# Three products of two tiles per f on GpSimd in an MLP of a hybrid encoder layer, and a later split of the first chunk's gated tiles

## The chip, the core and the metric

The kernel runs on one core of a Trainium2 chip. Five engines work side by side, each with its own queue of instructions that it takes in order: TensorE (PE, matmuls; PEld are its weight loads), VectorE (DVE), ScalarE (ACT), GpSimd (POOL) and SyncE (SP, which only issues DMAs here). They wait for each other through semaphores. The metric is the device time of one execution in microseconds (us).

## The reference

One encoder layer over 512 tokens of width 2048: a normalised input projection, a convolution group and a neighbourhood-attention group beside each other, an output projection, and then a gated MLP. The change touches the MLP alone:

```python
xn = rms_norm(x, ffn_norm_g[l])
up = jnp.einsum("bsd,df->bsf", xn, w_up[l])
up = depthwise_conv(up, ffn_dw_w[l], ffn_dw_b[l])     # width 3 over tokens
gate, val = jnp.split(up, 2, axis=-1)
x = x + jnp.einsum("bsf,fd->bsd", jax.nn.silu(gate) * val, w_down[l])
return rms_norm(x, final_norm_g)
```

D_FF is 5632, so `up` has 11264 columns. All data are float32.

## The kernel before

Everything is kept transposed: a tile has 128 channels as partitions and 512 tokens as columns. A float32 product is made of matmuls on a rounded high part and a low part of each operand (`hi`/`lo`, `hh`/`hl`): `mm3` (L122 to L127) issues high by high (L125), high by low (L126) and low by high (L127). For each weight unit of 128x1024, `parts` (L111) makes the high part on ACT (`whi`, L114) and the low part on DVE (`wlo`, L115); there are four buffers of each, and SP loads the raw units into seven buffers.

The MLP runs over f = 0 to 43 (`NF`), each f standing for 128 columns of gate and 128 of value. Four f make a chunk (`CH` = 4), so there are eleven chunks c. For each f, `up` (or `up_apart` in chunk 0) makes seven products, numbered 0 to 6, instead of eight, in the manner of Strassen-Winograd: the weights of a product are sums of the raw units (`factors`, DVE adds `ws`, L622 to L633), and the products are added up to g and v from PSUM (`pu`) on ACT and DVE (L684 are ACT's copies `vv` and `pl` out of a bank). Products 0 to 5 share three PSUM banks (`psm`), so product 3 takes the bank of product 0; product 6 has its own (`po`).

`hidden(f)` (L764) then multiplies g and v by the reciprocal norm `rstd2` (L766, L767), runs the convolution (`conv3`: L758 on ACT, L759 and L760 on DVE, each for g and v), the silu (L769, ACT), and the gated product (L770). `in_two` (L773) splits a gated tile into `hh` (L775, ACT) and `hl` (L776, DVE). The first three gated tiles of a chunk are split just before the last f of the chunk, the fourth at the end of the chunk.

A chunk's gated tiles go through the down projection during the next chunk: `up` calls `between` after each product, and after products 3 and 6 `down` (L779) multiplies the four tiles of the chunk before with a unit of down weights, two output tiles d at a time (`pd`). ACT copies each result out (`pdc`, L790) and GpSimd issues a DMA that adds it to `x2d` in DRAM (L791).

The order on each engine is not the order of the source. The program is written with priorities, and a scheduler with its own costs orders each engine's instructions when the kernel is built. Each engine then keeps to this fixed order, so an instruction that waits holds up all that stand behind it on its engine.

At the very end of the kernel four products of final tiles run on GpSimd (L839) beside DVE's (L841); until then GpSimd's work is DMA issues.

Of the kernel before, what the change touches and what calls it, by code (L numbers as in the profile page):

```python
# [41 lines left out]
CH = 4  # L42
# [23 lines left out]
def layer(ctx: ExitStack, tc: tile.TileContext, xT, w_in, w_out, w_up, w_down, par, tab, out):  # L66
    nc = tc.nc
# [16 lines left out]
    def t2(name, dt=F32):  # L84
        return tp.tile([P, S], dt, tag="t2k", name=name)
# [174 lines left out]
    for k in range(KD):  # L260
        x1.append(t2("x"))
        last = pin(nc.sync.dma_start(x1[k], xT[k]))
        h, l = t2("xh", F32R), t2("xl", F32R)
# [8 lines left out]
    for step in ORDER:  # L272
        i = next(a_ if step == "a" else q_)
# [323 lines left out]
    rstd2 = []  # L597
# [44 lines left out]
    def down_units(c, i, at):  # L642

        n = U // CH
        if not c:
            return ()
        if c < NCH - 1:
            return {3: (4 * i,), 6: (4 * i + n,)}.get(at, ())
        return {(1, 3): (0,), (1, 6): (2,), (2, 3): (4,), (2, 6): (6,), (3, 6): range(8, KD, n)}.get((i, at), ())
# [104 lines left out]
    def conv3(a, n):  # L754
        y = t2("uy")
        o = POFF["fww"] + 3 * n
        w, o = (prm, o) if n < NF else (fwn, o - POFF["fww"] - 3 * NF)
        nc.scalar.activation(y, a, AF.Identity, scale=w[:, o + 1:o + 2], bias=pc("fwb", n))  # L758
        nc.vector.scalar_tensor_tensor(y[:, 1:], a[:, :S - 1], w[:, o:o + 1], y[:, 1:], op0=ALU.mult, op1=ALU.add)  # L759
        nc.vector.scalar_tensor_tensor(y[:, :S - 1], a[:, 1:], w[:, o + 2:o + 3], y[:, :S - 1],  # L760
                                       op0=ALU.mult, op1=ALU.add)
        return y

    def hidden(f, between):  # L764
        g, v = (up_apart if f < CH else up)(f, between)
        nc.vector.tensor_mul(g, g, rstd2[0])  # L766
        nc.vector.tensor_mul(v, v, rstd2[0])  # L767
        g, v = conv3(g, f), conv3(v, NF + f)
        nc.scalar.activation(g, g, AF.Silu)  # L769
        nc.vector.tensor_mul(g, g, v)  # L770
        return g

    def in_two(g):  # L773
        h, l = t2("hh", F32R), t2("hl", F32R)
        nc.scalar.activation(h, g, AF.Copy)  # L775
        nc.vector.tensor_sub(l, g, h.bitcast(F32))  # L776
        return h, l

    def down(hs, ds, wide=False):  # L779

        for d0 in ds:
            w = weights()
            for d in range(d0, d0 + U // CH):

                ps = (psm.tile([P, S], F32, tag="mm", name="pd") if wide and d % 5 > 1 else
                      psa.tile([P, S], F32, tag="tr", name="pd", bufs=2))
                for k in range(CH):
                    mm3(ps, w, (d - d0) * CH + k, *hs[k], k == 0, k == CH - 1)
                t = t2("pdc")
                nc.scalar.activation(t, ps, AF.Copy)  # L790
                nc.gpsimd.dma_start(xd[d], t, accum_op=ALU.add)  # L791

    pend = None
    for c in range(NCH):
        hs = []
        for i in range(CH):

            last = c == NCH - 1 and i == CH - 1
            if i == CH - 1:
                hs = [in_two(h) for h in hs]  # L800
            hs.append(hidden(c * CH + i, lambda at: None if last else down(pend, down_units(c, i, at))))
        hs[-1] = in_two(hs[-1])
        if not last:
            pend = hs

# [141 lines left out]
```

## Time and profile before

| | us |
|---|---|
| three runs | 2051.95, 2054.8, 2055.14 |
| median | 2054.8 |
| the profiled execution, its own time | 2052.8 |
| its span, first to last instruction | 2051.0 |
| PE in the products of chunk 0 (f = 0 to 3), from the span's start | 682 to 766 |
| PE in those of chunks 1 to 10, with the down projection of chunks 0 to 9 | 766 to 1988 |

How to read what is shown of it. A row of the table of waits says which engine, writing which tile at which line, waited for which engine's tile: total us, times, longest. A row of a group says line, engine, operation, the tiles out<-in, shapes and count, then busy us and mean ns of one, then the engine's idle time ahead of them and what ended it. A row of the timeline begins with its start and duration in us; brackets at its end hold the idle time before it and what ended it. The row by windows has the length of the stretch and then, for PE, PEld, DVE, ACT and POOL, busy us and instructions, then the granted clock. `source` rows give min/median/max in ns. Matmuls are pipelined, so their durations overlap and the step from start to start tells their rate.

### The profile page before, as it was taken

What the parts mean: (1) busy time and instruction counts of PE and PEld (TensorE: products, weight loads), DVE (VectorE), ACT (ScalarE), POOL (GpSimd) and SP (SyncE); (2) the same over time, 40 slices, a digit from 0 to 9 for tenths busy, and PEclk for the clock granted to TensorE, in tenths of its full rate; (3) what the DMA queues carried; (4) which work ended last, traced back from release to release, by engine and by line L of the source; (5) the groups of instructions that cost most, each with busy time, mean ns of one, the idle gap of its engine ahead of it and who ended that gap; (6) DMA issues with size and microseconds to landing.
All of it is one profiled execution on the core that took longest, in us unless ns stands there. A gap on an engine that the chain in (4) does not pass through costs nothing.

```text
span 2051.0 us, 28588 instructions
## 1 busy us (share of the span) xinstructions
PE 2031.7 (99%) x10816; PEld 1736.7 (85%) x10816; DVE 1666.7 (81%) x2319; ACT 1060.8 (52%) x1726; POOL 156.2 (8%) x186
## 2 busy tenths in 40 slices
PE   9999999999999999999999999999999999999997
PEld 7888888888788998888888888888888888888887
DVE  7996697686577898888878878888888888889876
ACT  6244424457436555555555555555554555555562
POOL 0000000000001001111111111111111111110110
PEclk9999999999999999999999999999999999999999
DMA  7332333236237435555555565565565565555682
GB/s 253 113 103 83 99 98 111 84 103 237 82 118 184 119 116 130 135 149 136 129 147 141 128 145 143 129 143 144 124 144 144 124 150 141 136 129 134 147 212 83
DMA packets 97209, 275.38 MB, mean 134 GB/s; under 512 B 10928, under 2 KB 11696, under 8 KB 97072
## 3 DMA queue, kind: packets, MB, share of 16 engines
q1 hardware_dynamic: 71712, 227.40, 35.0%
q0 software_dynamic: 25216, 46.15, 14.8%
q8 instruction: 85, 1.39, 0.3%
q14 instruction: 52, 0.43, 0.1%
q10 hardware_dynamic: 144, 0.01, 0.0%
HBM read 218.99 MB, written 54.53 MB: 133 GB/s over the span
## 4 chain that ended last, share of the span: by engine, by line
PE 97%; DVE 1%; DMA 0%; issue 0%; ACT 0%; DVEq 0%; ACTq 0%
PE pu L672 25%; PE pu L677 13%; PE pd L127 8%; PE pd L125 8%; PE pd L126 8%; PE pj L125 7%; PE pj L127 7%; PE pj L126 7%; PE po L125 3%; PE po L127 3%; PE po L126 3%; PE pu L125 1%; PE pu L127 1%; PE pu L126 1%; PE sc L437 1%; PE po L476 1%
## 5 line engine op out<-in xcount | busy, mean ns | idle before, releaser
L114 ACT ACTIVATE whi<-raw 128x1024 fp32r<-128x1024 f32 x364 | 384.4, 1058 | 486.8 <-PE pj L126 178.5
L115 DVE TENSOR_TENSOR wlo<-raw,whi 128x1024 fp32r<-128x1024 f32 x364 | 444.3, 1222 | 221.4 <-ACT whi L114 198.8
L672 PE MATMUL pu<-xc,whi 128*128 128x512 f32 x2240 | 574.7, 392 | 0.0
L672 PEld LDWEIGHTS pu<-xc,whi 128*128 128x128 f32 x2240 | 409.1, 189 | 74.0 <-ACT pl L684 0.2
L677 PEld LDWEIGHTS pu<-xc,wlo 128*128 128x128 f32 x2240 | 305.6, 190 | 21.9
L677 PE MATMUL pu<-xc,wlo 128*128 128x256 f32 x2240 | 312.3, 282 | 0.0
L125 PE MATMUL pd<-hh,whi 128*128 128x512 f32 x640 | 249.0, 391 | 2.6 <-ACT hh L775 2.6
L125 PE MATMUL pj<-xh,whi 128*128 128x512 f32 x640 | 251.1, 396 | 0.0
L127 PE MATMUL pj<-xh,wlo 128*128 128x512 f32 x640 | 249.7, 390 | 0.0
L126 PE MATMUL pj<-xl,whi 128*128 128x512 f32 x640 | 249.7, 390 | 0.0
L126 PE MATMUL pd<-hl,whi 128*128 128x512 f32 x640 | 249.2, 389 | 0.0
L127 PE MATMUL pd<-hh,wlo 128*128 128x512 f32 x640 | 249.2, 391 | 0.0
L791 POOL DMA_DIRECT2D x2d<-pdc x160 | 139.3, 872 | 1167.7 <-ACT pdc L790 949.5
L684 ACT ACTIVATE pl<-pu 128x256 f32<-128x256 f32 x280 | 104.5, 382 | 166.0 <-PE pu L672 165.9
L114 ACT ACTIVATE whi<-ws 128x1024 fp32r<-128x1024 f32 x132 | 139.8, 1059 | 78.1 <-PE pu L672 57.9
L343 DVE SCALAR_TENSOR_TENSOR y<-ch,prm,y 128x504 f32<-128x504 f32 (+14 forms) x240 | 173.7, 742 | 4.6
L115 DVE TENSOR_TENSOR wlo<-ws,whi 128x1024 fp32r<-128x1024 f32 x132 | 161.0, 1220 | 19.8 <-ACT whi L114 19.7
L127 PEld LDWEIGHTS pd<-hh,wlo 128*128 128x128 f32 x640 | 120.1, 188 | 28.8 <-DVE wlo L115 3.0
L125 PEld LDWEIGHTS pj<-xh,whi 128*128 128x128 f32 x640 | 120.2, 188 | 27.9 <-issue 3.7
L127 PEld LDWEIGHTS pj<-xh,wlo 128*128 128x128 f32 x640 | 120.2, 188 | 25.9 <-DVE wlo L242 0.4
L126 PEld LDWEIGHTS pj<-xl,whi 128*128 128x128 f32 x640 | 120.4, 188 | 25.0 <-DVE xl L265 0.7
L125 PEld LDWEIGHTS pd<-hh,whi 128*128 128x128 f32 x640 | 120.5, 188 | 24.9 <-ACT hh L775 3.0
(182 smaller groups left out, 2742.9 us busy)
## 6 DMA issues: line engine op xcount, KB each, us to landing
raw<-in_w_up SPq DMA_DIRECT2D x176, 512.0 KB, 3.6
raw<-in_w_down SPq DMA_DIRECT2D x88, 512.0 KB, 3.7
x2d<-pdc POOLq DMA_DIRECT2D x160, 256.0 KB, 4.7
raw<-in_w_in SPq DMA_DIRECT2D x76, 512.0 KB, 3.7
raw<-in_w_out SPq DMA_DIRECT2D x32, 512.0 KB, 3.9
x<-in_xT SPq DMA_DIRECT2D x32, 256.0 KB, 5.3
tab<-in_tab SPq DMA_DIRECT2D x32, 256.0 KB, 5.2
x2d<-x SPq DMA_DIRECT2D x16, 256.0 KB, 2.1
```

What stands on the lines that cost most here:

```text
L114: i = nc.scalar.activation(hi[:, :n], raw[:, :n], AF.Copy)
L115: j = nc.vector.tensor_sub(lo[:, :n], raw[:, :n], hi[:, :n].bitcast(F32))
L125: nc.tensor.matmul(ps, hi[:, a], mh, start=start, stop=False)
L126: nc.tensor.matmul(ps, hi[:, a], ml, start=False, stop=False)
L127: return nc.tensor.matmul(ps, lo[:, a], mh, start=False, stop=stop)
L343: nc.vector.scalar_tensor_tensor(y[:, a:b], h[:, a + j - PAD:b + j - PAD], prm[:, o + j:o + j + 1], y[:, a:b], op0=ALU.mult, op1=ALU.add)
L437: m = nc.tensor.matmul(banks[b // 2 * 2 + j][:, b % 2, :], q[hp, b * P:(b + 1) * P], grid(k, KC0[b], KW)[hp], start=True, stop=True)
L476: m = nc.tensor.matmul(grid(po, b * BLK, BLK)[hp], vt[b // 2][:, 2 * (b % 2) + ch, hp], pts[b // 2 * 2 + j][:, 2 * (b % 2) + ch, :], start ...
L672: return nc.tensor.matmul(ps, w[0][:, k * P:(k + 1) * P], comb[c][k], start=k == 0, stop=k == U - 1)
L677: nc.tensor.matmul(ps[:, H:], w[1][:, k * P:(k + 1) * P], comb[c][k][:, :H], start=False, stop=False)
L684: nc.scalar.activation(to, ps, AF.Copy)
L791: nc.gpsimd.dma_start(xd[d], t, accum_op=ALU.add)
```

## The change

```diff
     def hidden(f, between):
         g, v = (up_apart if f < CH else up)(f, between)
-        nc.vector.tensor_mul(g, g, rstd2[0])
-        nc.vector.tensor_mul(v, v, rstd2[0])
+        mul = (nc.gpsimd if f >= CH and f % CH < CH - 1 else nc.vector).tensor_mul
+        mul(g, g, rstd2[0])
+        mul(v, v, rstd2[0])
         g, v = conv3(g, f), conv3(v, NF + f)
         nc.scalar.activation(g, g, AF.Silu)
-        nc.vector.tensor_mul(g, g, v)
+        mul(g, g, v)
         return g
...
         for i in range(CH):
 
             last = c == NCH - 1 and i == CH - 1
-            if i == CH - 1:
+            if c and i == CH - 1:
                 hs = [in_two(h) for h in hs]
             hs.append(hidden(c * CH + i, lambda at: None if last else down(pend, down_units(c, i, at))))
-        hs[-1] = in_two(hs[-1])
+        hs = [h if isinstance(h, tuple) else in_two(h) for h in hs]
         if not last:
             pend = hs
```

From f = 4 on, the two products with the norm and the gated product of an f run on GpSimd, except in the last f of a chunk, where they stay on DVE. That is 30 f and 90 products of 128x512. In chunk 0 all products stay on DVE, and the first three gated tiles are split at the end of the chunk together with the fourth. One line is added ahead of the products, so lines from L766 on have a number higher by one in the changed kernel.

The scheduler orders the changed program anew. PE has the same instructions; their order differs at ten places, after product 2 of the last f of chunks 1 to 9 and at the first down projection after chunk 0. At the nine, eight down matmuls stood between products 2 and 3, and now three do; the other five come after product 3. On ACT, the copies L684 of products 0 and 1 there now come directly behind the `hh` of the third gated tile, ahead of a `whi`. On GpSimd the products stand between the accumulations of `x2d`.

## The prediction

> **What bounds the kernel now.** I read the page first, then the table of PE's waits, then the groups by line and shape, then the timeline at the places that the waits point to. Times of the timeline are microseconds from the span's start.
>
> ```profile
> span 2051.0 us, 28588 instructions
> PE 2031.7 (99%) x10816; PEld 1736.7 (85%) x10816; DVE 1666.7 (81%) x2319; ACT 1060.8 (52%) x1726; POOL 156.2 (8%) x186
> PE 97%; DVE 1%; DMA 0%; issue 0%; ACT 0%; DVEq 0%; ACTq 0%
> ...
> PE pd L125 <- ACT hh L775: 2.6, 1, 2.6
> ...
> PEld pd L127 <- DVE wlo L115: 3.0, 9, 0.3
> ...
> 820.00:1960.00 1140.00, 1140.00 (x5997) 979.95 (x5996) 957.81 (x1210) 625.97 (x979) 127.05 (x146) 1.00 0.56 138
> ```
>
> PE sets the end: 97% of the chain is matmuls, and from 820 to 1960, which is nearly all of the MLP from f = 4 on, PE is busy for all of 1140 us at the full granted clock (1.00), while DVE works 957.81. DVE can therefore cost time only where PE waits for it. The waits name two such places in the MLP: once 2.6 us for a high part (hh) of a gated tile, and nine times for a low part of down weights (wlo). Nine is the number of full chunks after the first (c = 1 to 9). Whatever the change saves on DVE, no more can be won here than these two waits hold.
>
> The nine waits look alike. This is the one in the middle of chunk 3, where f%4 is 3:
>
> ```profile
> 1102.53 0.87 POOL L791 DMA_DIRECT2D x2d<-pdc  x1 [9.45 <-ACT pdc L790]
> ...
> 1105.11 1.23 DVE L115 TENSOR_TENSOR wlo<-raw,whi 128x1024 fp32r<-128x1024 f32 x1 [2.13 <-ACT whi L114]
> ...
> 1105.46 0.80 ACT L758 ACTIVATE uy<-g,prm 128x512 f32<-128x512 f32 x1
> ...
> 1110.03 0.74 DVE L760 SCALAR_TENSOR_TENSOR uy<-vl,fwn,uy 128x511 f32<-128x511 f32 x1
> ...
> 1110.69 0.68 DVE L776 TENSOR_TENSOR hl<-uy,hh 128x512 fp32r<-128x512 f32 x1
> ...
> 1111.29 0.69 DVE L770 TENSOR_TENSOR uy<-uy 128x512 f32<-128x512 f32 x1
> 1111.89 1.22 DVE L115 TENSOR_TENSOR wlo<-raw,whi 128x1024 fp32r<-128x1024 f32 x1
> 1112.01 0.64 ACT L775 ACTIVATE hh<-uy 128x512 fp32r<-128x512 f32 x1 [0.97 <-DVE uy L770]
> ...
> 1112.41 0.40 PE L125 MATMUL pd<-hh,whi 128*128 128x512 f32 x1
> ...
> 1112.61 1.06 ACT L114 ACTIVATE whi<-raw 128x1024 fp32r<-128x1024 f32 x1
> 1112.64 0.39 PE L126 MATMUL pd<-hl,whi 128*128 128x512 f32 x1
> ...
> 1113.17 0.50 PE L127 MATMUL pd<-hh,wlo 128*128 128x512 f32 x1
> ...
> 1113.57 0.36 ACT L684 ACTIVATE vv<-pu 128x256 f32<-128x256 f32 x1
> ...
> 1113.84 0.37 ACT L684 ACTIVATE pl<-pu 128x256 f32<-128x256 f32 x1
> ...
> 1114.43 0.63 PE L672 MATMUL pu<-xc,whi 128*128 128x512 f32 x2
> ```
>
> PE runs eight down matmuls (pd) here between product 2 and product 3 of an f. They step by 0.23 (1112.41 to 1112.64), so eight take 1.84; they took 2.02 (to 1114.43), because L127 waited for the wlo that ended at 1113.11. The stall is 0.18 at each border, 1.6 over nine. Two more things matter below. Product 3 needs the bank of product 0, which ACT frees with the two L684 copies at 1113.57 and 1113.84 (done 1114.21, only 0.22 before PE takes it); and these copies stand behind hh in ACT's queue.
>
> The single wait is the border after chunk 0:
>
> ```profile
> 766.18 1.22 DVE L115 TENSOR_TENSOR wlo<-raw,whi 128x1024 fp32r<-128x1024 f32 x1
> ...
> 767.42 7.23 SPq L109 DMA_DIRECT2D raw<-in_w_up  x2
> ...
> 771.94 1.23 DVE L622 TENSOR_TENSOR ws<-raw 128x1024 f32<-128x1024 f32 x1 [1.33 <-DMA raw<-in_w_up]
> ...
> 774.38 0.40 PE L125 MATMUL pd<-hh,whi 128*128 128x512 f32 x1
> ...
> 776.20 0.75 DVE L760 SCALAR_TENSOR_TENSOR uy<-vl,fwn,uy 128x511 f32<-128x511 f32 x1
> ...
> 776.44 0.39 PE L125 MATMUL pd<-hh,whi 128*128 128x512 f32 x1
> ...
> 779.40 0.50 PE L125 MATMUL pd<-hh,whi 128*128 128x512 f32 x1 [2.57 <-ACT hh L775]
> ```
>
> PE stood from 776.67 to 779.40, 2.73 us. The end of an L115 frees the buffer whose load starts at 767.42; L622 waits for that load, and the convolution and the last gated tile queue behind L622.
>
> **The change part by part.** *Removed from DVE.* Thirty f (three in each of chunks 1 to 10) lose three products each:
>
> ```profile
> L766 DVE TENSOR_TENSOR g<-g,rstd 128x512 f32<-128x512 f32 x44 | 30.4, 691 | 1.3
> L770 DVE TENSOR_TENSOR uy<-uy 128x512 f32<-128x512 f32 x44 | 30.2, 686 | 0.1
> ...
> L839 POOL TENSOR_TENSOR fin<-x,rb x4: 718/720/726, 2042.2 to 2044.3; 128x256 f32<-128x256 f32 x4
> ...
> L841 DVE SCALAR_TENSOR_TENSOR fin<-x,prm,rb 128x256 f32<-128x256 f32 x12 | 4.8, 476 | 0.9 <-PE rb L201 0.9
> ...
> L722 DVE TENSOR_TENSOR g<-vv,pu 128x256 f32<-128x256 f32 x40 | 16.6, 415 | 0.0
> ```
>
> 90 x 0.69 = 62 us less for DVE, worth nothing by itself under a PE that is busy throughout.
>
> *Added to GpSimd.* No row has a 128x512 product there. At 128x256 it takes 0.72. DVE's own pair, 415 ns at 256 and 690 at 512, has a fixed part of 140; with that, GpSimd gets 0.14 + 2 x 0.58 = 1.30. Bounds: 0.72 (all of it fixed) and 1.44 (none). I take 1.30: 90 of them add 117 us to 127 us of work in a stretch of 1140, so GpSimd does not become the bound.
>
> *Where GpSimd's products wait and who waits for them.* In GpSimd's queue the product of g stands behind one x2d accumulation: free at 1103.40, done at 1104.70, and ACT's L758, its reader, starts only at 1105.46. So this is covered by 0.76, without interference. The product of v comes earlier still. DVE idles 2.13 just before 1105.11, which takes up one delay of 1.30. The x2d issues that queue behind a product go out up to 1.3 later; the next accumulation on the same x2d is a chunk away.
>
> *The third product at a border.* The gated products of f%4 = 0 and 1 are split only when f%4 is 3, a whole f or more later. That of f%4 = 2 (L770) has a reader at once: hh on ACT, and behind hh the two copies that free product 0's bank. The built order of the changed kernel also differs here: wlo follows hl directly, PE runs only three down matmuls before product 3 instead of eight, and ACT has the copies right behind hh, with whi after them. So PE wants wlo at 1112.41 + 2 x 0.23 = 1112.87 and product 0's bank at 1113.10, over a microsecond earlier than now. GpSimd can start when L760 ends, 1110.77, plus the 0.03 that lie between L770's end and hh now: 1110.80. From its end to the freed bank go 0.03, then 0.60 and 0.27 from start to start and 0.37 for the copy: 1.27.
>
> - Without interference: it ends at 1112.10, the bank is free at 1113.37, the stall is 0.27 against 0.18 now: +0.09 x 9 = +0.8. With 1.44 instead of 1.30, +2.2; with 0.72 no stall, -1.6.
> - Taking turns: DVE's instructions there, hl and wlo, each read two tensors in SBUF, back to back. If the two engines do not overlap on those, the product waits for hl (1111.37) and ends at 1112.67; wlo runs after it, to 1113.89, and L127 starts at 1113.95 instead of 1112.87: a stall of 1.08, or +0.90 x 9 = +8.1. The copies are done at 1113.94, just in time.
> - Turns lost: DVE's wlo goes first (1111.29 to 1112.51); the product ends at 1113.81, the bank is free at 1115.08, the stall is 1.98, +1.8 x 9 = +16.2.
>
> No row shows such a pair. The one overlap in the trace, L839 beside L841, shows none (four products within 718 to 726 ns, and 476 ns for DVE's twelve, of which about half ran alone), but L841 reads a single tensor from SBUF, the other from PSUM. Every DVE instruction near L770's new place reads two from SBUF, as the product itself does, so that row is no witness for them, and I take the middle case, +8.1.
>
> The Trainium skill, page "SBUF — State Buffer", section "Who interferes with whom", speaks against this change: a VectorE instruction with two SBUF inputs contends with a GpSimd instruction that reads SBUF, and the second to issue is blocked until the first is done. By that rule the sum is one of the two latter cases; no run here shows it yet.
>
> *The first chunk's splits.* Three splits (hh on ACT, hl on DVE) go from before the last f of chunk 0 to behind it; nothing is added. DVE is without a gap before 766.18, so 3 x 0.69 = 2.06 less work brings that L115 forward. I take 1.8 of it, as the L115 also needs ACT's high part, and move the load and L622 with it. L760 then ends near 775.15; the first hl, which PE wants at 774.84, is done at 775.75 (0.9 late). The third hl comes after L770, the second hl and one L115, near 778.7, against 778.5 wanted (0.2 late). PE's changed order runs 16 matmuls instead of 10 before the last hh. Stalls of 1.1 replace 2.73: -1.6. Bounds: 0, if the load comes no earlier, and -2.7.
>
> *Sum*, against the profiled execution's own 2052.8 (span 2051.0 and 1.8 around it; the median shown is 2054.8, 0.1% more): 2052.8 - 1.6 + 8.1 = **2059.3 us**, 0.3% slower.
>
> **The rivals.** (1) No interference: 2052.8 - 1.6 + 0.8 = 2052.0, no change; not slower. For it: L839 beside L841. It decides from the point where the product ends by 1112.2. (2) A gain: the product is quick (0.72) and the border after chunk 0 recovers: 2052.8 - 1.6 - 1.6 = 2049.6, at best 2048.5. Against it: it needs all of GpSimd's 0.72 to be fixed. (3) Turns lost at every border: 2052.8 - 1.6 + 16.2 = 2067.4. Against it: GpSimd would have to be passed over at the end of hl.
>
> **How the numbers follow.** Forecast 0.43, rival 1 0.33, rival 2 0.10, rival 3 0.14. A measurement of this kernel can tell about 0.2% (4 us) from no change. The forecast and rival 3 are slower, less 0.05 for a turn that costs only half: 0.52. Faster by over 4 us needs rival 2 at its best or a lucky reading of it: 0.10. The rest, 0.38, is no change. The forecast's own range is 2056 to 2062; as the cases have both signs, the range goes from rival 2 to rival 3, 2049.5 to 2068.
>
> **What would show it.** If I am right: nine PE stalls of about 1 us, each ended by DVE's wlo at L127, and DVE instructions beside a GpSimd product start late or last longer by up to 1.3. If rival 1 is: GpSimd products of 1.3 beside undisturbed DVE, and nine waits of 0.3 for ACT's pl copy at product 3. For rival 3: products over 2 us long and waits of 2. The hh wait at 779 should shrink to about 1 and move to hl. GpSimd products far over 1.44 with no DVE work beside them, or a new wait elsewhere than at the borders, would make the prediction wrong.

## The result and the profile after

| | before | after |
|---|---|---|
| median of five runs each, us | 2054.43 | 2073.5 |
| lowest and highest | 2051.95, 2055.14 | 2070.15, 2076.16 |
| ratio of the times, 95% interval | | 1.0093 (1.0079 to 1.0106) |
| the profiled execution, its own time | 2052.8 | 2073.5 |

The change costs 0.9%. In the rows of the changed kernel the norm products are L767 and L768, the gated product is L771, `hh` is L776 and `hl` L777.

From the page of the changed kernel, the span, the busy times and the chain of work that ended last; then its row by windows for the same stretch as before:

```profile
span 2071.7 us, 28640 instructions
PE 2035.5 (98%) x10816; PEld 1738.3 (84%) x10816; DVE 1644.8 (79%) x2229; ACT 1058.7 (51%) x1726; POOL 328.0 (16%) x276
PE 91%; DVE 4%; ACT 1%; POOL 1%; issue 1%; DMA 1%; DVEq 0%; POOLq 0%; ACTq 0%
```

```profile
820.00:1960.00 1140.00, 1124.91 (x5910) 966.03 (x5910) 922.93 (x1105) 613.50 (x960) 285.75 (x229) 1.00 0.58 136
```

DVE is busy for 22 us less, not for the 62 that were taken from it, and GpSimd for 172 more. PE, which was busy for all of these 1140 us, now is for 1124.91, at the same clock: 15 us of idle time have come in. The table of waits says where:

```profile
PE pu L672 <- ACT pl L684: 17.5, 11, 2.4
PE pd L126 <- DVE hl L777: 2.1, 1, 2.1
...
ACT hh L776 <- POOL uy L771: 26.6, 10, 2.8
```

The nine waits for wlo are gone. In their place PE waits eleven times for the `pl` copy, that is for the bank of product 0, and ACT waits ten times for the gated product on GpSimd before it can make `hh`. This is the border in chunk 3 again, from the timeline:

```profile
1114.18 0.68 DVE L777 TENSOR_TENSOR hl<-uy,hh 128x512 fp32r<-128x512 f32 x1
1114.41 2.72 POOL L771 TENSOR_TENSOR uy<-uy 128x512 f32<-128x512 f32 x1 [4.08 <-DVE uy L760]
...
1114.78 1.21 DVE L115 TENSOR_TENSOR wlo<-raw,whi 128x1024 fp32r<-128x1024 f32 x1
...
1116.36 0.40 PE L127 MATMUL pd<-hh,wlo 128*128 128x512 f32 x1
1117.16 0.63 ACT L776 ACTIVATE hh<-uy 128x512 fp32r<-128x512 f32 x1 [2.63 <-POOL uy L771]
1117.70 0.36 ACT L684 ACTIVATE vv<-pu 128x256 f32<-128x256 f32 x1
...
1117.96 0.38 ACT L684 ACTIVATE pl<-pu 128x256 f32<-128x256 f32 x1
...
1118.39 1.67 PE L672 MATMUL pu<-xc,whi 128*128 128x512 f32 x6 [1.64 <-ACT pl L684]
```

The product starts at 1114.41, while hl runs. hl ends at 1114.86, but wlo starts and runs its 1.21 undisturbed; the product ends at 1117.13, 1.14 after wlo does (1115.99). hh follows 0.03 later, the two copies behind it, and product 3 starts 1.64 after PE had run out of work. From this border to the next takes 1242.09 - 1118.39 = 123.70 us now, where it took 1236.39 - 1114.43 = 121.96:

```profile
1242.09 0.74 PE L672 MATMUL pu<-xc,whi 128*128 128x512 f32 x2 [1.65 <-ACT pl L684]
```

and in the kernel before

```profile
1236.39 0.85 PE L672 MATMUL pu<-xc,whi 128*128 128x512 f32 x3
```

So a border costs 1.74, and nine of them 15.7. The last chunk's border costs more. GpSimd's product there lasts 4.44, PE stands for 2.36, and for 3.3 us its granted clock is 0.50:

```profile
1968.30 4.44 POOL L771 TENSOR_TENSOR uy<-uy 128x512 f32<-128x512 f32 x1 [2.37 <-ACT uy L770]
...
1973.99 0.80 PE L672 MATMUL pu<-xc,whi 128*128 128x512 f32 x1 [2.36 <-ACT pl L684]
```

```profile
1973.60:1976.90 3.30, 2.91 (x7) 2.33 (x8) 3.27 (x6) 2.22 (x6) 0.00 (x0) 0.50 0.22 25
```

20.7 lie between the two profiled executions; 15.7 are the nine borders, and of the 5 that are left about 3.9 are chunk 10's, as a run below shows. The last microsecond is not assigned.

### The profile page after: what moved, and what is told of

Its sections match the earlier page's. It is cut to its first block, busy times and chain, and to the rows that moved or that the text cites. A ratio compares the mean times of both kernels' runs of the same rounds, so it can differ in the third digit from the quotient of the medians.

```text
span 2071.7 us, 28640 instructions
## 1 busy us (share of the span) xinstructions
PE 2035.5 (98%) x10816; PEld 1738.3 (84%) x10816; DVE 1644.8 (79%) x2229; ACT 1058.7 (51%) x1726; POOL 328.0 (16%) x276
## 4 chain that ended last, share of the span: by engine, by line
PE 91%; DVE 4%; ACT 1%; POOL 1%; issue 1%; DMA 1%; DVEq 0%; POOLq 0%; ACTq 0%
PE pu L672 22%; PE pu L677 11%; PE pd L126 8%; PE pd L125 8%; PE pd L127 7%; PE pj L125 7%; PE pj L127 7%; PE pj L126 7%; PE po L125 3%; PE po L126 3%; PE po L127 3%; POOL uy L771 1%; PE pu L125 1%; PE pu L127 1%; PE pu L126 1%
## 5 line engine op out<-in xcount | busy, mean ns | idle before, releaser
L672 PE MATMUL pu<-xc,whi 128*128 128x512 f32 x2240 | 577.7, 393 | 17.5 <-ACT pl L684 17.5
L672 PEld LDWEIGHTS pu<-xc,whi 128*128 128x128 f32 x2240 | 409.4, 189 | 95.4 <-ACT pl L684 22.0
L127 PE MATMUL pj<-xh,wlo 128*128 128x512 f32 x640 | 250.0, 391 | 0.0
L127 PE MATMUL pd<-hh,wlo 128*128 128x512 f32 x640 | 248.2, 390 | 0.0
L115 DVE TENSOR_TENSOR wlo<-ws,whi 128x1024 fp32r<-128x1024 f32 x132 | 173.0, 1311 | 27.2 <-ACT whi L114 27.0
L684 ACT ACTIVATE pl<-pu 128x256 f32<-128x256 f32 x280 | 104.0, 381 | 142.1 <-PE pu L672 142.1
L126 PEld LDWEIGHTS pd<-hl,whi 128*128 128x128 f32 x640 | 120.2, 188 | 28.2 <-DVE hl L777 2.9
L127 PEld LDWEIGHTS pj<-xh,wlo 128*128 128x128 f32 x640 | 120.3, 188 | 26.2 <-DVE wlo L242 0.7
L127 PEld LDWEIGHTS pd<-hh,wlo 128*128 128x128 f32 x640 | 120.1, 188 | 26.0
```

Of the source, the lines that this page charges most:

```text
L115: j = nc.vector.tensor_sub(lo[:, :n], raw[:, :n], hi[:, :n].bitcast(F32))
L126: nc.tensor.matmul(ps, hi[:, a], ml, start=False, stop=False)
L127: return nc.tensor.matmul(ps, lo[:, a], mh, start=False, stop=stop)
L672: return nc.tensor.matmul(ps, w[0][:, k * P:(k + 1) * P], comb[c][k], start=k == 0, stop=k == U - 1)
L684: nc.scalar.activation(to, ps, AF.Copy)
```

## The experiments

Theory "lock": at a border the third product, now on GpSimd, is passed over by DVE's hl and wlo; hh on ACT waits for it, behind hh the two bank copies, and behind these product 3. Rivals: DVE is slowed everywhere by 90 products on GpSimd; PE's new order (three down matmuls ahead of product 3 instead of eight) costs it; a 128x512 product on GpSimd simply takes 2.7 us. The kernels, with the ratio to the kernel before on the same chip:

| kernel | median, us | ratio (95%) |
|---|---|---|
| third product back on DVE, 80 on GpSimd | 2052.69 | 0.9992 (0.9983 to 1.0001) |
| third product alone on GpSimd, 80 on DVE | 2072.77 | 1.0090 (1.0076 to 1.0104) |
| chunk 0's later split alone | 2052.84 | 0.9996 (0.9987 to 1.0005) |
| changed kernel, third tile split late | 2052.10 | 0.9989 (0.9980 to 0.9998) |
| changed kernel, PE's old order at the borders | 2064.00 | 1.0042 (1.0027 to 1.0057) |
| third product on DVE, PE's new order | 2062.27 | 1.0040 (1.0024 to 1.0056) |
| changed kernel, chunk 10 on DVE | 2068.03 | 1.0069 (1.0053 to 1.0085) |
| late split alone, all on DVE | 2052.04 | 0.9984 (0.9975 to 0.9993) |
| changed kernel, product starts earlier | 2072.88 | 1.0091 (1.0074 to 1.0108) |
| changed kernel, a gap on DVE at the borders | 2060.41 | 1.0030 (1.0018 to 1.0041) |

### The third product: undone, and alone

```diff
-        mul(g, g, v)
+        (nc.vector.tensor_mul if f % CH == CH - 2 else mul)(g, g, v)
```

> The changed kernel with one thing undone: the gated product of f%4 = 2 is back on DVE (ten products); the other 80 products stay on GpSimd, and so does the later split of chunk 0. Theory 'lock' (the GpSimd product at a border is passed over by DVE's hl and wlo, and hh, the two bank copies and product 3 wait for it): all of the loss goes, 2054 us, ratio to the kernel before 1.000 (0.998 to 1.001), no PE waits for the pl copy over 1 us, GpSimd's L771 still over 2 us at f%4 = 0 and 1. Rival 'DVE slowed everywhere' (90 GpSimd products make DVE's instructions longer, and this adds up): most of the loss stays, 2068 to 2073, ratio 1.007 to 1.009. Rival 'order' (PE takes product 3 after three down matmuls instead of eight): not told apart here, since the old order on PE comes back with this edit.

In the kernel before, with nothing else of the change:

```diff
-        nc.vector.tensor_mul(g, g, v)
+        (nc.gpsimd if f >= CH and f % CH == CH - 2 else nc.vector).tensor_mul(g, g, v)
```

> The kernel before with one thing of the change alone: the gated product of f%4 = 2 on GpSimd, in chunks 1 to 10 (ten products). Theory 'lock': all of the loss is here: nine PE stalls of 1.8 us and about 5 us at chunk 10's border, 2073 to 2075 us, ratio 1.009 to 1.010. Rival 'DVE slowed everywhere': ten products of 90 leave at most a ninth of the loss, 2055 to 2057, ratio 1.000 to 1.001. Rival 'order': as 'lock', since PE's new order comes with this edit.

Ten products of 90 carry all of the loss: 2072.77 with them alone, 2052.69 with the 80 others. The waits of the first kernel, and then of the second, show the same:

```profile
PEld pd L127 <- DVE wlo L115: 3.0, 9, 0.3
```

```profile
ACT hh L775 <- POOL uy L770: 26.5, 10, 2.8
...
PE pu L672 <- ACT pl L684: 17.1, 10, 2.4
```

The first has the nine small waits for wlo that the kernel before has. That DVE is slowed everywhere falls as the cause. The other gated products on GpSimd are as slow in the first kernel, as this row shows, and its DVE works 1650.7 us, 16 less than the 1666.7 of the kernel before, though 80 products of 0.69, 55 us, were taken from it. But PE hardly waits for any of that:

```profile
L771 POOL TENSOR_TENSOR uy<-uy x20: 2452/2712/8332, 805.0 to 1922.6; 128x512 f32<-128x512 f32 x20
```

### The third tile's split moved

```diff
             if c and i == CH - 1:
-                hs = [in_two(h) for h in hs]
+                hs = [in_two(h) for h in hs[:2]] + hs[2:]
```

> The changed kernel, but the third gated tile of a chunk is split at the end of the chunk, with the fourth; all 90 products stay on GpSimd. hh then no longer stands ahead of the two bank copies on ACT. Theory 'lock': the GpSimd product still takes 2 to 3 us at the border, but nobody waits for it at once, so the time comes back to 2053 to 2057 us, ratio 0.999 to 1.001; a small wait may come at the end of the chunk, where two splits now stand together. Rival 'DVE slowed everywhere': 2068 to 2073, as GpSimd has the same products. Rival 'slow product' (a 128x512 product on GpSimd takes 2.7 us by itself): the same time as by 'lock', but L771 would be near 2.7 us wherever it runs, also where DVE is idle or has PSUM inputs.

All 90 products stay on GpSimd, the third is even later, and the loss is gone (2052.10). The timeline at the border in chunk 3:

```profile
1110.95 7.87 POOL L771 TENSOR_TENSOR uy<-uy 128x512 f32<-128x512 f32 x1 [4.07 <-DVE uy L760]
```

```profile
1111.31 1.22 DVE L115 TENSOR_TENSOR wlo<-raw,whi 128x1024 fp32r<-128x1024 f32 x1
...
1116.46 1.21 DVE L624 TENSOR_TENSOR raw<-raw 128x1024 f32<-128x1024 f32 x1
1117.66 2.24 DVE L115 TENSOR_TENSOR wlo<-ws,whi 128x1024 fp32r<-128x1024 f32 x1
```

GpSimd's product takes 7.87 here, six DVE instructions go before it, and PE is busy for all of the 1140 us from 820 to 1960, as in the kernel before. So GpSimd's slowness by itself costs nothing; what costs time is who waits for it: hh ahead of the copies on ACT. The scheduler changed PE's order here too: product 3 follows product 2 with no down matmul between. It does not wait all the same, as the copies of product 0's bank are done at 1111.61 and PE comes to product 3 only at about 1112.4.

The same split with every product on DVE, in the kernel before:

```diff
-            if i == CH - 1:
-                hs = [in_two(h) for h in hs]
+            if c and i == CH - 1:
+                hs = [in_two(h) for h in hs[:2]] + hs[2:]
...
-        hs[-1] = in_two(hs[-1])
+        hs = [h if isinstance(h, tuple) else in_two(h) for h in hs]
```

> The late split alone: all products on DVE as before, the third gated tile of a chunk split at the end of the chunk with the fourth, and chunk 0's four tiles there too. If the 62 us taken from DVE are worth nothing under PE, this is as fast as the kernel with the late split and 90 products on GpSimd (2052.1): 2051 to 2053, ratio to before 0.998 to 1.000. If GpSimd's products bring something of their own, it is slower than that one by over 2 us.

2052.04 against 2052.10, with ratios of 0.9984 and 0.9989: the 62 us taken from DVE bring nothing that can be measured under a PE that is busy throughout, as the prediction had it. The late split by itself has the lowest ratio of the table, 0.16% under the kernel before (0.07 to 0.25); that is about what the nine waits of 0.18 and a part of the one after chunk 0 would give, but its interval overlaps with those of three other rows.

### PE's order

In the changed kernel, product 3's first matmul (`firsts`) is tied behind the eighth of the down matmuls (`downs`, from number n on) that stand around it:

```diff
+                if 0 < c < NCH - 1 and i == CH - 1 and at == 3:
+                    tc.add_manual_dep(firsts[c * CH + i, 3].ins, downs[n + 7].ins.name,
...
```

> The changed kernel with PE's order of before at the nine borders: product 3 is held behind eight down matmuls again (five more than in the changed kernel); all 90 products stay on GpSimd. Theory 'lock': the copies behind hh come as late as in the changed kernel, but five more matmuls of 0.23 fill 1.15 of each wait of 1.81: nine stalls of 0.7 are left, and chunk 10's border (about 5 us) is as it was: 2073.5 - 9 x 1.15 = 2063, 2061 to 2066, ratio 1.004 to 1.006. Rival 'order' (product 3's earlier place alone makes the loss): the nine stalls go, 2053 to 2059.

And in the first kernel of the table, which has the third product on DVE, the down matmuls from the fourth on are tied behind product 3:

```diff
+                    for later in downs[n + 3:]:
+                        tc.add_manual_dep(later.ins, firsts[c * CH + i, 3].ins.name,
...
```

> The first experiment (gated product of f%4 = 2 on DVE, the other 80 on GpSimd) with PE's order of the changed kernel at the nine borders: product 3 behind three down matmuls. Theory 'lock': the bank copies are done in time or nearly so, stalls of 0 to 1 us at a border by the trace of before (ACT still has a whi ahead of the copies, which cost it 1.06 there: the bank is free at 1114.21 against 1113.10 wanted, so about 0.9 net x 9 = 8 if that whi stays there): 2053 to 2062. Rival 'order': 9 x 1.8 as in the changed kernel, 2068 to 2070.

These kernels have other line numbers: L676 is product 3, L690 the copies, L129 the matmul with wlo. The timeline of the first at two borders, and of the second at the same two:

```profile
993.15 1.20 PE L676 MATMUL pu<-xc,whi 128*128 128x512 f32 x4 [0.52 <-ACT pl L690]
...
1115.70 0.96 PE L676 MATMUL pu<-xc,whi 128*128 128x512 f32 x3 [0.52 <-ACT pl L690]
```

```profile
991.15 0.73 PE L676 MATMUL pu<-xc,whi 128*128 128x512 f32 x2 [0.59 <-ACT pl L690]
...
1114.17 0.50 PE L676 MATMUL pu<-xc,whi 128*128 128x512 f32 x1 [0.59 <-ACT pl L690]
```

From border to border: 122.55 with GpSimd and the old order, 123.02 with DVE and the new one, against 121.96 before and 123.70 with both. A border thus costs 0.59, 1.06 and 1.74. Neither part makes the loss alone. The late product costs 0.59 even where five more matmuls cover it; five of 0.23 are 1.15, just what lies between 0.59 and 1.74. The second kernel costs 1.06 with a quick product, and its 2062.27 is 0.3 above what was expected at most. But that is not the price of PE's order alone: a `whi` of 1.06 still stands ahead of the copies there, which the changed kernel does not have. And the kernels with the late split have product 3 in a still earlier place and lose nothing. So "order" is part of the cause in this way: the new order takes 1.15 of cover from product 3, and that counts because the copies are late. The change brings both, and both are in its nine borders.

### Chunk 10

```diff
-        mul = (nc.gpsimd if f >= CH and f % CH < CH - 1 else nc.vector).tensor_mul
+        mul = (nc.gpsimd if CH <= f < NF - CH and f % CH < CH - 1 else nc.vector).tensor_mul
```

> The changed kernel with chunk 10's nine products back on DVE; 81 stay on GpSimd. Theory: chunk 10's border costs about 5 us, half by its own stall of 2.5 us and half by a granted clock of 0.5 for 3.4 us behind it: 2073.5 - 5 = 2068.5, ratio 1.006 to 1.008, and no stretch at a clock below 0.9 near the end of the products. If the clock's fall had another cause: the half clock stays and only 2.5 us or less are won, 2071 or more.

As expected: 2068.03, and the stretch of its last products runs without a stop at the full clock. From product 3 at the ninth border to the start of the last L672 matmul this kernel takes 1980.6 - 1858.72 = 121.9, and the changed kernel 1986.4 - 1860.57 = 125.8. The 3.9 between them are the 2.36 of waiting and about 1.5 for 2.91 us of work at half the clock.

```profile
1966.00:1986.00 20.00, 20.00 (x111) 17.40 (x110) 18.94 (x28) 11.73 (x20) 0.00 (x0) 1.00 0.61 178
```

### Chunk 0's border

In the kernel before, without a product moved:

```diff
-            if i == CH - 1:
+            if c and i == CH - 1:
...
-        hs[-1] = in_two(hs[-1])
+        hs = [h if isinstance(h, tuple) else in_two(h) for h in hs]
```

> The kernel before with the later split of chunk 0's gated tiles alone; all products on DVE. By the trace of the changed kernel: the load behind L115 starts 1.3 us earlier but lands only 0.3 earlier, so the gain is 0.3 us, 2054.1, ratio 0.9999. By the prediction's term: -1.6 us, 2052.8, ratio 0.9992. PE's wait there: for hl, 2.0 to 2.6 us (trace of the changed kernel) against about 1.1 (prediction).

2052.84 is 1.3 under its neighbour of before; the interval (0.9987 to 1.0005, or 2.7 less to 1.0 more) can't tell this from either value, nor from nothing. The profile speaks for the prediction's: PE waits 0.9 for hl there.

```profile
PE pd L126 <- DVE hl L776: 0.9, 1, 0.9
```

What the trace of the changed kernel shows (2.1) goes with a late load: L622 waits 2.38 for it, and only 1.19 (to 770.01) with the later split alone.

```profile
771.65 1.23 DVE L622 TENSOR_TENSOR ws<-raw 128x1024 f32<-128x1024 f32 x1 [2.38 <-DMA raw<-in_w_up]
```

Over the nine kernels here with the later split and the changed one that wait was 0.2 to 2.1, about 1.0 in the mean. In the two without it, it was 2.6 (the kernel before) and 1.7 (the third product alone).

### Who goes first: GpSimd or DVE

The prediction's middle case had the two engines take turns. This is the pair by itself, its case B, written out without the helper functions (`pin` keeps the order of the source):

```python
pin(nc.vector.tensor_sub(yb, gate, b))
for k in range(8):
    pin(nc.vector.tensor_sub(los[k], wide, wide2))
for k in range(2):
    pin(nc.gpsimd.tensor_mul(outs[k], yb, b))
```

> The disputed pair by itself; the layer is left out, the output is a copy of a scratch tile. Products of 128x512 on GpSimd: (A) alone; (B) ready under a row of eight back-to-back DVE instructions of 128x1024 with two inputs in SBUF; (C) ready under a row of eight with one input in PSUM; (D) under way when DVE instructions with two inputs in SBUF come; (E) those DVE instructions alone; (F) beside DVE instructions between which DVE waits for ACT. Theory 'lock': A 1.4 to 1.6 us; B not done before the row ends, 8 to 11 us; C 1.4 to 1.6; D the DVE instructions start or last up to 1.6 longer and the products near 1.5 or taking turns; E 1.22 each; F each product done in a gap, under 3 us. Rival 'taking turns' (the prediction's): B at most one DVE instruction of delay, 1.2 + 1.5 = 2.7 us. Rival 'slow product': A 2.7 us.

The rows of the products by group, then the timeline of case B:

```profile
L93 POOL TENSOR_TENSOR uy<-gate,b x15: 1261/1707/2237, 10.0 to 62.8; 128x512 f32<-128x512 f32 x15
...
L93 POOL TENSOR_TENSOR uy<-yb,b x2: 2110/2174/2238, 16.5 to 18.5; 128x512 f32<-128x512 f32 x2
L93 POOL TENSOR_TENSOR uy<-ye,b x2: 1264/1266/1267, 29.8 to 31.1; 128x512 f32<-128x512 f32 x2
```

```profile
16.22 1.22 DVE L98 TENSOR_TENSOR lo<-wide,wide 128x1024 fp32r<-128x1024 f32 x1
16.45 2.11 POOL L93 TENSOR_TENSOR uy<-yb,b 128x512 f32<-128x512 f32 x1 [1.53 <-DVE yb L109]
...
17.36 2.28 DVE L98 TENSOR_TENSOR lo<-wide,wide 128x1024 fp32r<-128x1024 f32 x1
```

Alone a product takes 1.26 (the shortest of the first row), which is near the 1.30 estimated; "slow product" falls. Beside a DVE with an input in PSUM (the row with ye) it takes 1.27. Under DVE's row with two inputs in SBUF it waits for the instruction in progress, to 17.44, ends 1.12 after it, and the next DVE instruction waits: 2.28 is 1.06 of waiting and 1.22 of work. That is strictly taking turns, not the lock of the layer's trace; by this the prediction's middle case would have been right. In the layer the same product was passed over at every border. Three runs looked for what makes the difference; they vary the lines above as their texts say.

> What decides who gets the turn; the layer is left out, the output is a copy of a scratch tile. In each phase a GpSimd product becomes ready at the end of a DVE instruction, under a row of five more of 128x1024 with two SBUF inputs. (a) plain; (b) product in place; (c) a half-length DVE instruction (0.69) is the one in progress, as hl is at the border; (d) each DVE instruction waits for a load that landed long ago; (e) the product stands behind a DMA issue in GpSimd's queue; (f) half-length, behind a DMA issue, in place; (g) as f, with loads; (h) as c again. The plain phase should take one turn, as in the earlier run of the pair: done at the end of the first DVE instruction plus 1.12, 2.1 us in all. Idea 'half length' (GpSimd asks for its turn only some 0.5 to 0.9 us after its start): c, f, g and h lose one turn (2.7 us), the others none. Idea 'queue': only e, f and g lose. Idea 'waits': only d and g lose, and more than one turn (up to 7 us). If none loses, something else in the layer decides, and it stays open.

> What of the layer makes GpSimd lose its turn; the layer is left out, the output is a copy of a scratch tile. Each phase has a half-length DVE instruction in progress, then a row of five of 128x1024 with two SBUF inputs, as at a border, and one product that becomes ready under it: (a, j) control; (b) TensorE matmuls running; (c) ScalarE copies running; (d) DVE's inputs as wlo's, a raw unit and a high part that ScalarE wrote; (e) the product's tiles at the top of SBUF, 60 KB or more above DVE's; (f) DVE's tiles there too; (g) b, c, d and e together; (h) loads running; (i) b, c, e and h together. Control: the next turn, 1.6 us. If one of these is what the layer adds, the phases that have it take 2.7 us or more (up to 6, the row's end). If all take 1.6, none of them is it, and the cause of the lost turn stays open.

> Once more what of the layer makes GpSimd lose its turn, this time by how DVE's row looks; the layer is left out, the output is a copy of a scratch tile. One product under a half-length DVE instruction and a row of five: (a, h) control; (b) TensorE reads what each DVE instruction of the row writes; (c) the product becomes ready in the middle of DVE's row, behind five instructions back to back; (d) the product reads a tile that ScalarE wrote beside the one that DVE wrote; (e) the instruction before is the convolution's; (f) b and c; (g) all of them. Control: the next turn, 1.6 us. What takes 2.7 or more is what the layer adds; if all take 1.6, the cause stays open.

In all of their 26 phases the product took the next turn (1.6 us behind a half-length instruction, 2.2 behind a whole one). For one, the product of the last run that becomes ready in the middle of DVE's row:

```profile
42.59 0.68 DVE L104 TENSOR_TENSOR lo<-wide,wide 128x512 fp32r<-128x512 f32 x1
42.75 1.65 POOL L111 TENSOR_TENSOR uyc<-yc,b 128x512 f32<-128x512 f32 x1 [12.42 <-DVE yc L103]
```

It starts 0.16 after the DVE instruction in progress; the products at the borders start 0.24 after. Two runs tested whether that decides, one in the layer and one in the pair alone. In the layer the gated product was written over v, with a product of one column ahead of it:

```diff
...
+        if mul == nc.gpsimd.tensor_mul:
+            nc.gpsimd.tensor_mul(scr, g[:, :1], rstd2[0][:, :1])
-        mul(g, g, v)
-        return g
+        mul(v, g, v)
+        return v
```

> The changed kernel with a GpSimd product that starts earlier: a product of one column ahead of the gated product waits for the silu in its place, and the gated product is written over v, so that it waits for two semaphores instead of three (about 0.1 us less between L760's end and its start). Everything else is as in the changed kernel. Idea 'start': in the traces so far GpSimd got the next turn where it started up to 0.23 us after the start of the DVE instruction in progress, and was passed over where it started later (0.24 at the borders). Started at 0.14, it takes the turn after hl and ends 1.13 after it; wlo is done 1.1 later than now, so PE waits some 0.8 for wlo and 0.1 for the copy: about 1.0 in place of 1.92 at nine borders, and chunk 10's border loses most of its 5: 2073.5 - 8 - 5 = 2060, 2057 to 2065, with a wait for wlo at L127 nine times. If the start doesn't decide: 2071 to 2075, products of 2.7 as before.

> When does a product take its turn; the layer is left out, the output is a copy of a scratch tile. As in the second run of the pair, but with one, two or three semaphores to wait for ahead of the product, so that it starts some 0.16, 0.25 and 0.33 us after the DVE instruction in progress: (a, b, c, j) with a half-length DVE instruction in progress, (d, e, f) with one of full length, (g, h, i) with a gap in DVE's row after two or three instructions (a DVE instruction of one column that waits for the one before it). Idea 'start': a and d (one wait) take the next turn and are done 1.13 after the instruction in progress; those that start over 0.235 after it are passed over to the end of the row (6 us), or to the gap in g, h and i (2.7 to 4 us). If the start doesn't decide: all take the next turn, 1.6 (half) or 2.2 us (full).

The start does not decide. In the layer the product now starts at 0.16 and is passed over all the same (hl is L781, the product L775):

```profile
1112.77 0.68 DVE L781 TENSOR_TENSOR hl<-uy,hh 128x512 fp32r<-128x512 f32 x1
1112.93 2.79 POOL L775 TENSOR_TENSOR uy<-uy 128x512 f32<-128x512 f32 x1 [0.69 <-DVE uy L760]
1113.37 1.22 DVE L115 TENSOR_TENSOR wlo<-raw,whi 128x1024 fp32r<-128x1024 f32 x1
```

and in the pair alone a product that starts 0.23 after takes its turn all the same (1.58). Later starts, of 0.25 and 0.33, were meant there, but none of its ten products came later than 0.23, so it is the run in the layer that settles this.

### A gap gives the turn back

In the changed kernel DVE got an instruction of one column between the second hl and wlo, which must wait for that hl:

```diff
...
         nc.vector.tensor_sub(l, g, h.bitcast(F32))
+        if gap:
+            nc.vector.tensor_sub(scr, l[:, :1].bitcast(F32), l[:, 1:2].bitcast(F32))
```

(and the wlo that follows is tied behind it).

> The changed kernel with a gap on DVE at the borders: between the second hl and wlo, DVE gets an instruction of one column that has to wait for the hl just written. The GpSimd product starts as late as in the changed kernel. Idea 'gap': a product that was passed over gets its turn at the first gap (in the changed kernel L633, which comes 0.03 after L115's end, waited for GpSimd 20 times): product done 1.13 after hl, wlo 1.2 later than now, about 1.0 lost at each of nine borders in place of 1.92, chunk 10's border much less than 5: 2057 to 2065. Rival 'the product is always a whole instruction late': 2071 to 2075.

Its waits, and the border in chunk 3 (here hl is L787, the added instruction L789, wlo L117, the matmul with wlo L135):

```profile
PE pd L135 <- DVE wlo L117: 6.3, 9, 0.7
```

```profile
1111.46 0.69 DVE L787 TENSOR_TENSOR hl<-uy,hh 128x512 fp32r<-128x512 f32 x1
1111.70 1.60 POOL L779 TENSOR_TENSOR uy<-uy 128x512 f32<-128x512 f32 x1 [4.08 <-DVE uy L768]
...
1112.18 1.13 DVE L789 TENSOR_TENSOR scr<-hl 128x1 f32<-128x1 f32 x1
...
1113.24 1.22 DVE L117 TENSOR_TENSOR wlo<-raw,whi 128x1024 fp32r<-128x1024 f32 x1
...
1114.51 0.50 PE L135 MATMUL pd<-hh,wlo 128*128 128x512 f32 x1 [0.70 <-DVE wlo L117]
```

The product starts 0.24 after hl, as in the changed kernel, but hl is followed by a short pause: it gets the turn and takes 1.60. Now it is DVE that waits (1.13 for one column), wlo is late, and PE waits nine times at L127's place for it. One more instruction on DVE makes the changed kernel 13 us faster, 2060.41.

A pause is not the only way in, though. In the kernel with the third tile's split moved, one product in the first f of chunk 10 got the next turn in a row without a pause: it ends 1.16 after the wlo in progress, and L699, which has two inputs in SBUF, lasts 1.79 instead of 0.68.

```profile
1894.38 1.21 DVE L115 TENSOR_TENSOR wlo<-ws,whi 128x1024 fp32r<-128x1024 f32 x1
...
1894.91 1.84 POOL L771 TENSOR_TENSOR uy<-uy 128x512 f32<-128x512 f32 x1 [4.18 <-ACT uy L770]
...
1895.51 1.79 DVE L699 TENSOR_TENSOR vv<-vv,pl 128x512 f32<-128x512 f32 x1
```

So the layer mostly passes the product over, and not always.

## Why the prediction was wrong

- *What bounds the kernel* was right. PE sets the end, and DVE's 62 us are worth nothing (2052.10 and 2052.04 with and without).
- *The place* was right. The third product at nine borders, with its chain of hh, copies and bank and with PE's three down matmuls, is where the time went; undone, it all comes back.
- *The step that failed* is the choice among the three cases: "I take the middle case, +8.1". The third happened, "turns lost": "DVE's wlo goes first", the product ends over a microsecond after wlo (1.14), and the price was nearly as worked out there, 1.8 a border predicted and 1.74 measured. Its condition, "GpSimd would have to be passed over at the end of hl", was held against it, and it is what the trace shows at each border.
- *The price of the middle case* was about right too: with the gap that makes the engines take turns there are nine waits for wlo, and from border to border (product 3 at 1115.07 and 1237.79) 122.72, which is 0.76 more than before where 0.90 was forecast. That the time, 2060.41, comes so near to the 2059.3 forecast is in part chance, as that kernel has an instruction more. The sum holds, for a case that did not occur.
- *The choice rested on* there being no row of two SBUF inputs beside GpSimd. That was so. Between two bounds with no row to decide, 0.14 for the worse one was too little, and the range ended at 2068.
- *A second step failed: chunk 10's border* was not priced, and it cost about 3.9 us. The step counted nine borders, because before the change nine had a wait. The tenth has the same product and the same hh, a longer DVE row, and no down matmuls to cover it. Without this term even the case of the lost turns ended at 2067.4.
- *The first chunk's splits*, -1.6: not contradicted, and not shown by the times either (-1.3 with that edit alone, with an interval that holds 0). The waits of the traces speak for it, about 1.0 in the mean against 2.6 and 1.7, though not in the profiled execution of the changed kernel, where the load came late.
- *GpSimd's product*, 1.30: 1.26 alone. In the layer the 30 products at L768, L767 and L771 took 1.41, 1.61 and 2.92 in the mean, 178 us instead of 117, and still GpSimd did not become the bound.
- *Two small terms*: the product was taken to start 0.03 after L760, and at the border above it starts 0.15 after it (1114.26 to 1114.41). And 1.44 in the case without interference gives 9 x 0.23 = +2.1, not +2.2. Nothing hangs on either.

The Trainium skill, page "SBUF — State Buffer", section "Who interferes with whom", says that the ports which the two engines share are an exclusive lock, that issue order decides which of the two blocks, and that a DVE instruction with at most one input in SBUF does not contend. The pair by itself agrees (2.11 and 2.28, and 1.27 with an input in PSUM). The layer's trace does not agree on the order: a product that started 0.37 before wlo ended 1.14 after it.

Not settled is why DVE's row mostly keeps its turn in the layer and never did in the pair alone. The product's start does not decide (passed over at 0.16 in the layer, not at 0.23 in the pair). None of the following made the product lose its turn when it was added to the pair: waits, a DMA issue ahead of it, writing in place, the other engines and loads beside it, places in SBUF, readers of DVE's tiles and a row that is already running. What the runs do show is that at the borders a pause on DVE lets the product in.

## What to carry to other kernels

Before work is moved to a slower or shared engine, look at who waits for its result and what stands behind that reader in its queue: ten products of 90 cost everything here, because hh stood ahead of two bank copies, and with that hh behind them the same products cost nothing. Relief for DVE gained nothing here, as its work was under PE's throughout. And where two mechanisms are open and no row decides, price each at every place where it can occur, the ends of a loop among them, and let the range hold the worse one.

## What the runs showed of the hardware that was not expected

In the layer a GpSimd product under back-to-back DVE instructions with two inputs in SBUF can wait for six of them (7.87 us for 1.3 of work), and a DVE instruction of one column lasted 1.13 when it came behind such a product.

PE's granted clock was 0.50 for 3.3 us after an idle time of 2.36 (the rows of chunk 10 above), though it stayed at 1.00 after one of 2.08 in the same execution:

```profile
777.31 0.50 PE L126 MATMUL pd<-hl,whi 128*128 128x512 f32 x1 [2.08 <-DVE hl L777]
```

```profile
776.80:780.00 3.20, 2.69 (x12) 2.17 (x12) 3.20 (x5) 3.20 (x8) 0.00 (x0) 1.00 0.07 29
```

In the kernel with PE's old order it was 0.50 after an idle time of 1.87, in the first f of chunk 10:

```profile
1881.75 1.21 PE L676 MATMUL pu<-xc,whi 128*128 128x512 f32 x2 [1.87 <-ACT pl L690]
```

```profile
1881.80:1884.60 2.80, 2.80 (x7) 2.25 (x8) 2.77 (x5) 1.78 (x4) 0.00 (x0) 0.50 0.24 20
```

The Trainium skill, page "TensorE: Matmul & The Clock Gate", section "What's actually happening", puts the fall after at least one idle window of about 3.4 us; in these two places less was enough. In chunk 10 the 2.91 us of work at half the clock lost about 1.5 more (an estimate, half of them): a wait of 2.36 on PE cost 3.9.
